# One layer of a recurrent and attention encoder in float32: all eight column tiles of the up projection's first half in Strassen quads

## The chip, the core and the metric

The kernel runs on one core of a Trainium2 chip. The metric is device time in microseconds of one execution, as the median of several runs. Five engines run side by side, each with its own queue of instructions in program order: TensorE (PE in the profile; its weight loads are PEld), VectorE (DVE), ScalarE (ACT), GpSimd (POOL) and SyncE (SP). An engine waits where it depends on another engine's result, on a transfer, or on a buffer that is still in use. SP issues the plain transfers of weights from device memory. POOL issues the accumulating ones, in which the DMA engines add the block that they read to what the destination holds.

## What is computed

The reference, cut to the part around the change (S = 512 tokens, D = 1024, D_FF = 4096, float32):

```python
x = x + concat(rms_norm(y_rnn), rms_norm(y_attn)) @ w_out     # w_out: 1024 x 1024
h = rms_norm(x, mlp_norm_g)
x = x + jnp.square(jax.nn.relu(h @ w_up)) @ w_down            # 1024 x 4096, 4096 x 1024
return rms_norm(x, final_norm_g)
```

Ahead of it stand the input projection, a gated linear recurrence in both directions, and a dilated attention of eight heads.

## The kernel before

**Split arithmetic.** Each float32 operand of a product is split in two fp32r numbers, `hi`, the rounded value, and `lo`, the remainder. `mm3` (lines 328 to 331) makes a product of three matmuls, hi*hi, hi*lo, lo*hi. For a weight chunk of 128x1024 the split is a cast `whi<-wraw` or `whi<-tw` on ACT (`conv_hi`, L274) and a subtraction `wlo<-...` on DVE (`conv_lo`, L282).

**The MLP.** It is computed in two halves of D_FF. Half 0's up projection (matmuls into `pu`) is followed by its down projection (into `pd`), then half 1's. An up half has 16 column tiles of 128, numbered f0. A plain column tile (`n0` to `n3`) takes eight contraction steps k of three matmuls of 128x512, all tokens, and one weight chunk. A quad f0 covers the four column tiles from f0 on by Strassen's scheme in Winograd's form: weights and activations are cut in blocks 11, 12, 21, 22 (two column groups by two halves of the contraction, two halves of the tokens), and seven products named `11`, `21`, `22`, `t1`, `t2`, `t3`, `t4` stand for eight. Each product is one weight chunk and 24 matmuls of 128x256. The operands t1 to t4 are sums of weight blocks: t1 = 12 + 11, t2 = t1 + 22, t3 = 12 + 22, t4 = t2 + 21 (signs are folded into the stored blocks). They are held in buffers `tw`. On the activation side the sums `hsum` stand against them, made from `hm`, the normed and transposed activations, and split to `hh` and `hl`; the activations themselves are split to `h2h` and `h2l`. Half 0 is four plain tiles and the quads 4, 8 and 12; half 1 is four quads (0, 8, 12, 4).

**What sets the order.** `STEPS` (L52) writes out the order of tiles and products in each half; chunks of weights follow it. During the step of chunk c, `feed` and `feed_q` cast and split chunk c+3, so ACT, DVE and TensorE run through the same list at a distance. In every quad but the first of half 0, `swap` converts t1 ahead of 11. A split frees the raw weights, and `conv_lo` then issues what may use that buffer next: `emit_dma` a plain load on SP into one of three `wraw` buffers, or, on POOL, the accumulation of 22 onto t1's buffer, which makes it t2 (L294). Where t3's or t4's sum needs the raw chunk 22 or 21, DVE adds it in place (L298, L303). `load_t` (L1196) takes one of four `tw` buffers, issues a plain load of block 12 on SP and the accumulations on POOL; its calls stand in `late`, a table of (f0, kind, n) that says beside which matmul group of which step something is done. `late` also places the activation sums, their splits (`split_h`), the squares of the residual stream for the final norms (`xt`, calling `x1_sq`), and `scale_neg`, which makes the negated norm factors `nr2`.

**Results of products.** `quad_evac` copies some products from PSUM to `v` on ACT (L1394) and adds later ones to them on DVE, `a<-v,pu` (L1404); relu and square follow on ACT or DVE. TensorE may start a product in a PSUM bank only when the one before it in that bank has been read. Products 11, t2, t3 and t4 of a quad share a bank.

**Start of half 0.** The output projection (into `pwo`) ends in `x1n<-pwo` on DVE (L1222). `h2_t` transposes `x1n` on TensorE into `pxt`, four 128x128 blocks for each k, ACT copies them to `h2h` and `hm`, DVE makes `h2l` (L1238). k = 0 to 3 stand before half 0's first product; k = 4 to 7 stand inside the first three plain tiles, which are interleaved.

Of the kernel before, what the change touches and what calls it, by code (L numbers as in the profile page):

```python
# [17 lines left out]
P = 128  # L18
# [23 lines left out]
for _n, _w in (("ag", 8), ("w0", 4), ("w1", 4), ("w2", 4), ("w3", 4), ("cb", 4),  # L42
# [13 lines left out]
ON_ACT = {(h, f, k) for h in range(2) for f in QUADS[h] if (h, f) != (0, 4) for k in ("21", "22", "t3", "t4")}  # L56

# [6 lines left out]
def up_steps(h):  # L64
    return [("n", int(s[1:])) if s[0] == "n" else (s.split(":")[1], int(s.split(":")[0])) for s in STEPS[h].split()]
# [44 lines left out]
def hybrid_kernel(ctx: ExitStack, tc, xw, xn, w_in, w_v, w_out, w_up, w_dn, gates, vecs, rel, onehot, fg, out):  # L110
# [165 lines left out]
    def conv_lo(i):  # L276
        if i < len(chunks):
# [13 lines left out]
            elif isinstance(c, tuple) and len(c) == 4:  # L291
# [4 lines left out]
                elif kind == "22":  # L296
                    t = raws[cq[h, f0, "t3"]]
                    nc.vector.tensor_tensor(t, t, r, op=OP.add)  # L298
                elif kind in ("t2", "21"):
# [896 lines left out]
    def load_t(half, n, f0):  # L1196
        t = work.tile([P, 1024], FT, name="tw", tag="tw", bufs=4)
        nc.sync.dma_start(t, ublock(half, "12", f0))
        for b in {"t1": ("11",), "t2": ("11", "22"), "t3": ()}[n]:
            nc.gpsimd.dma_start(t, ublock(half, b, f0), accum_op=OP.add)  # L1200
# [65 lines left out]
    BES["s1"].update({1: lambda: h2_t(0, "pj"), 2: lambda: h2_t(1, "pj"), 3: lambda: (conv_lo(C_WA + 8), h2_l(0))})  # L1266
    BES["22"].update({1: lambda: h2_t(2, "pj"), 2: lambda: (h2_t(3, "pj"), conv_lo(C_WA + 9)), 3: lambda: (h2_l(1), h2_l(2), h2_l(3))})
    for w in OSEQ:
# [7 lines left out]
        if w in ("s3", "s4", "s1"):  # L1276
            load_t(0, {"s3": "t1", "s4": "t2", "s1": "t3"}[w], 4)
# [4 lines left out]
    r2 = {}  # L1282

    def x1_sq(tt, n):
        s = small("ssn", 1)
        scr = g_("scr")
        act(scr, x1n[tt, n], AF.Square, accum_out=s)
        ssn[tt, n] = s
        if n == 1:
            r = consts.tile([P, 1], FT, name="r2_%d" % tt)  # L1290
            nc.vector.tensor_tensor(r, ssn[tt, 0], s, op=OP.add)
            nc.vector.tensor_scalar(r, r, 1.0 / D, EPS, op0=OP.mult, op1=OP.add)
            nc.vector.reciprocal(r, r)
            r2[tt] = r
# [35 lines left out]
    def up_evac(ff, p):  # L1330
        q, c = ff // 2, slice((ff % 2) * TH, (ff % 2 + 1) * TH)
        for t in range(2):
            if (q, t) not in rb:
                rb[q, t] = g_("a")
            act(rb[q, t][:, c], p[:, t * TH:(t + 1) * TH], AF.Relu)
        if ff % 2:
            for t in range(2):
                nc.vector.tensor_tensor(rb[q, t], rb[q, t], rb[q, t], op=OP.mult)
                rb_done.add((q, t))
            up_pair(q)  # L1340


# [5 lines left out]
    def h_sums(k):  # L1348
        m, c = k // 2, slice((k % 2) * TH, (k % 2 + 1) * TH)
        if k % 2 == 0:  # L1350
            for n in SUMS:
                hsum[n, m] = g_("hsum")
        a, b = hm.pop(k), hm.pop(k + 4)
        e, s2, s3, s4 = [hsum[n, m][:, c] for n in SUMS]
        nc.vector.tensor_tensor(e, b[:, right], a[:, right], op=OP.subtract)
        stt(s2, a[:, left], -1.0, e, op0=OP.mult, op1=OP.subtract)
        nc.vector.tensor_tensor(s3, a[:, left], a[:, right], op=OP.subtract)
        stt(s4, b[:, left], -1.0, s2, op0=OP.mult, op1=OP.subtract)
        if k % 2:
            for i, n in enumerate(SUMS):  # L1360
                nc.sync.dma_start(hsd[i][:, m * S:(m + 1) * S], hsum[n, m])
# [161 lines left out]
    nr2 = {}  # L1523
    for half in range(2):
        c0, cd = cu.get((half, 0)), cd_[half]
# [4 lines left out]
        start = 0  # L1530
        if half == 0:
            start = 3
            pu = [ps_("pu", "pj") for _ in range(start)]
            for k in range(KD):
                if k == 1:
                    for j in range(4, 8):
                        h2_t(j, "et" if j < 6 else "gs")
                        h2_l(j)
                for i in range(start):
                    mm3(pu[i], wk(c0 + i, k), h2k(k), k == 0, k == KD - 1)  # L1540
                    if i == 0:
# [12 lines left out]
            conv_hi(c0 + 5)
            conv_lo(c0 + 5)
            up_evac(2, pu[2])
        def scale_neg():
            nonlocal ts
            ts = big.tile([P, NQ, 1024], FT, name="ts", tag="bigA")
            for tt in range(4):  # L1560
                nr2[tt] = consts.tile([P, 1], FT, name="nr2_%d" % tt)
                nc.vector.tensor_scalar(nr2[tt], r2[tt], -1.0, None, op0=OP.mult)
# [5 lines left out]

        def up_tile(ff, late=()):
            p = ps_("pu", "pj")  # L1570
            c = cu[half, ff]
            for k in range(KD):
                mm3(p, wk(c, k), h2k(k), k == 0, k == KD - 1)
                feed(c, k)
                if (ff, k) in late:
                    late[ff, k]()
                if k in (1, 3, 5, 7):
                    op_next()
                if k in (5, 7):
                    next_a()  # L1580
            up_evac(ff, p)
# [3 lines left out]
        def up_step(kind, f0, late):  # L1585
            bank, keep = banks.setdefault(f0, {}), keeps.setdefault(f0, {})
            x = {"t1": "c", "22": "c", "21": "b"}.get(kind, "a")
            if x not in bank:
                bank[x] = ps_("pu", {"a": "pj" if (half, f0) == (1, 0) else "gs", "b": "pj", "c": "et"}[x])
            c = cq[half, f0, kind]  # L1590
            hi, lo = splits[c]
            for n in range(8):
# [9 lines left out]
                if n in (5, 7):  # L1602
                    op_next()
                if n == 6:
                    next_a()
            quad_evac(kind, f0, bank, keep, (half, f0, kind) in ON_ACT)

# [19 lines left out]
        for f0, f1 in zip(qs, qs[1:]):  # L1627
            late[f0, "t2", 0] = lambda f1=f1: load_t(half, "t1", f1)
            late[f0, "22", 0] = lambda f1=f1: load_t(half, "t3", f1)
        if half == 0:  # L1630
            late.update({(4, "11", 0): split_h("t2", 0), (4, "11", 5): split_h("t2", 1), (4, "t1", 1): split_h("22", 0), (4, "t1", 6): split_h("22", 1),
                         (3, 1): split_h("t3", 0), (3, 6): split_h("t3", 1),
# [183 lines left out]
```

## Time and profile before

| | |
|---|---|
| median of 3 runs | 531.61 us (530.47 to 531.9) |
| profiled execution | 532.29 us, span 530.5 us |
| busy, share of the span | TensorE 98%, DVE 81%, ACT 68%, POOL 13% |
| mean granted clock of TensorE | 0.997 of full speed |
| moved by DMA | 108.30 MB, mean 204 GB/s |
| accumulating transfers of w_up | 15 of 512 KB, median 8.3 us from issue to landing |

The span runs from the first to the last instruction; the 1.8 us beside it are start and end of the execution. A row of an engine's groups gives line, operation, output and inputs, shape and count, then busy time and mean duration of one in ns, then idle time ahead of it and what ended that. In rows of matmuls durations overlap, since they are pipelined. In a windows row stand, behind the stretch: its length and TensorE's busy time with count, then busy time and count of the weight loads, DVE, ACT and POOL, the granted clock, the DMA engines' busy share and GB/s. In timeline rows the first number is the start in us, the second the length; a number in brackets is a wait and what ended it.

### The profile page before, as it was taken

To read this page: it belongs to the slowest core of one execution; us is meant where nothing else is said; L and a number is where in the kernel's file an instruction comes from. 1 tells how busy PE (TensorE), PEld (TensorE's weight loads), DVE (VectorE), ACT (ScalarE), POOL (GpSimd) and SP (SyncE) were. 2 spreads that over 40 slices of the span, in tenths; PEclk is the share of its full clock that TensorE was granted. 3 is DMA by queue.
4 is the path that set the end of the run, shared out by engine and by line. 5 is a ranking of instruction groups with operands and counts; after the bars stand their busy time and mean duration, and the time that the engine had idled before them with its cause. 6 is when DMAs were issued, how large, how long until landed. Compare 5 with 4: busy or idle time off the path is not lost.

```text
span 530.5 us, 9181 instructions
## 1 busy us (share of the span) xinstructions
PE 521.1 (98%) x3495; PEld 446.4 (84%) x3495; DVE 431.0 (81%) x710; ACT 361.1 (68%) x569; POOL 66.8 (13%) x96
## 2 busy tenths in 40 slices
PE   8999999999999999999999999999999999999995
PEld 7855888877777878899999888888999999888884
DVE  5799589588779898898779986879756987987885
ACT  7566968578678867586477755575567677655654
POOL 3340000000202121001210222001101200131000
PEclk9999999999999999999999999999999999999998
DMA  8798165585567989948395999986968496799704
GB/s 309 256 236 217 41 152 159 164 150 179 105 220 153 331 196 256 371 146 229 100 214 144 228 272 274 311 289 140 291 209 228 107 223 207 163 299 263 174 1 159
DMA packets 35740, 108.30 MB, mean 204 GB/s; under 512 B 4109, under 2 KB 7082, under 8 KB 35696
## 3 DMA queue, kind: packets, MB, share of 16 engines
q1 hardware_dynamic: 26000, 74.66, 41.1%
q0 software_dynamic: 8784, 31.76, 32.1%
q10 hardware_dynamic: 912, 1.30, 1.3%
q8 instruction: 27, 0.44, 0.3%
q14 instruction: 17, 0.14, 0.1%
HBM read 98.24 MB, written 4.21 MB: 193 GB/s over the span
## 4 chain that ended last, share of the span: by engine, by line
PE 92%; ACT 2%; DMA 2%; DVE 2%; SPq 1%; issue 0%; DVEq 0%; ACTq 0%
PE pu L331 10%; PE pu L330 10%; PE pu L329 10%; PE pd L330 10%; PE pd L331 10%; PE pd L329 9%; PE pqk L329 3%; PE pqk L331 3%; PE pqk L330 3%; PE pt L841 2%; PE pav L928 2%; PE pv L329 1%; PE pn L787 1%; PE pp L331 1%; PE pp L329 1%; PE pp L330 1%
## 5 line engine op out<-in xcount | busy, mean ns | idle before, releaser
L282 DVE TENSOR_TENSOR wlo<-wraw,whi 128x1024 fp32r<-128x1024 f32 x72 | 87.8, 1221 | 26.4 <-ACT whi L274 26.2
L274 ACT ACTIVATE whi<-wraw 128x1024 fp32r<-128x1024 f32 x69 | 72.9, 1058 | 41.1 <-PE pd L331 20.5
L330 PE MATMUL pd<-wlo,ah 128*128 128x512 f32 (+1 forms) x195 | 75.4, 386 | 0.0
L329 PE MATMUL pd<-whi,ah 128*128 128x512 f32 (+1 forms) x195 | 75.3, 386 | 0.0
L331 PE MATMUL pd<-whi,al 128*128 128x512 f32 (+1 forms) x195 | 75.3, 386 | 0.0
L274 ACT ACTIVATE whi<-tw 128x1024 fp32r<-128x1024 f32 x40 | 42.3, 1059 | 38.0 <-DMA tw<-in_w_up_dram 11.1
L331 PE MATMUL pu<-hh,wlo 128*128 128x256 f32 x224 | 63.5, 284 | 0.0
L330 PE MATMUL pu<-hl,whi 128*128 128x256 f32 x224 | 63.5, 284 | 0.0
L329 PE MATMUL pu<-hh,whi 128*128 128x256 f32 x224 | 63.5, 283 | 0.0
L282 DVE TENSOR_TENSOR wlo<-tw,whi 128x1024 fp32r<-128x1024 f32 x40 | 48.9, 1223 | 17.9 <-ACT whi L274 17.9
L329 PE MATMUL pu<-h2h,whi 128*128 128x256 f32 (+1 forms) x200 | 60.2, 301 | 0.0
L331 PE MATMUL pu<-h2h,wlo 128*128 128x256 f32 (+1 forms) x200 | 60.1, 301 | 0.0
L330 PE MATMUL pu<-h2l,whi 128*128 128x256 f32 (+1 forms) x200 | 60.1, 301 | 0.0
L329 PEld LDWEIGHTS pu<-hh,whi 128*128 128x128 f32 x224 | 43.1, 192 | 0.0
L330 PEld LDWEIGHTS pu<-hl,whi 128*128 128x128 f32 x224 | 43.1, 192 | 0.0
L331 PEld LDWEIGHTS pu<-hh,wlo 128*128 128x128 f32 x224 | 43.1, 192 | 0.0
L329 PEld LDWEIGHTS pd<-whi,ah 128*128 128x128 f32 x195 | 36.7, 188 | 7.4
L330 PEld LDWEIGHTS pd<-wlo,ah 128*128 128x128 f32 x195 | 36.6, 188 | 7.3
L331 PEld LDWEIGHTS pd<-whi,al 128*128 128x128 f32 x195 | 36.7, 188 | 7.3
L274 ACT ACTIVATE whi<-ts 128x1024 fp32r<-128x1024 f32 x24 | 25.5, 1061 | 24.7 <-PE pd L331 18.5
L330 PEld LDWEIGHTS pu<-h2l,whi 128*128 128x128 f32 x200 | 38.3, 192 | 1.3
L331 PEld LDWEIGHTS pu<-h2h,wlo 128*128 128x128 f32 x200 | 38.3, 192 | 1.3
(286 smaller groups left out, 1232.8 us busy)
## 6 DMA issues: line engine op xcount, KB each, us to landing
wraw<-in_w_up_dram SPq DMA_DIRECT2D x25, 512.0 KB
ts<-in_w_dn_dram POOLq DMA_DIRECT2D x24, 512.0 KB, 13.5
wraw<-in_w_dn_dram SPq DMA_DIRECT2D x24, 512.0 KB
tw<-in_w_up_dram SPq DMA_DIRECT2D x15, 512.0 KB
tw<-in_w_up_dram POOLq DMA_DIRECT2D x15, 512.0 KB, 8.3
wraw<-in_w_in_dram SPq DMA_DIRECT2D x13, 512.0 KB
ts<-in_w_dn_dram SPq DMA_DIRECT2D x8, 512.0 KB
tw<-in_w_dn_dram SPq DMA_DIRECT2D x8, 512.0 KB
```

The lines of the kernel that those rows point to most:

```text
L274: act(hi, raws[i], AF.Copy)
L282: nc.vector.tensor_tensor(lo, r, f(splits[i][0]), op=OP.subtract)
L329: nc.tensor.matmul(o, lhsT=a[0], rhs=b[0], start=bool(first), stop=False, skip_group_check=on)
L330: nc.tensor.matmul(o, lhsT=a[0], rhs=b[1], start=False, stop=False, skip_group_check=on)
L331: nc.tensor.matmul(o, lhsT=a[1], rhs=b[0], start=False, stop=bool(last), skip_group_check=on)
L787: nc.tensor.matmul(pnear[p][e][r, o:o + k1 - k0], lhsT=q, rhs=raw[p, 1][halves[e], k0:k1], start=u == u0, stop=True, skip_group_check=True)
L841: nc.tensor.transpose(pt[:, i * P:(i + 1) * P], en[h][u][:, c * P:(c + 1) * P], ident)
L928: nc.tensor.matmul(o(half[e]), lhsT=v[:, h * DH:(h + 1) * DH], rhs=c(et[h, x]), start=first, stop=last, skip_group_check=True)
```

## The change

Half 0's plain column tiles go. In their place stands a quad 0, so that half 0 is four quads, 0, 4, 8 and 12:

```diff
 STEPS = (
-    "n0 n1 n2 4:11 4:t1 n3 4:t2 4:21 4:22 4:t3 8:11 8:t1 4:t4 8:t2 8:21 8:22 8:t3 12:11 12:t1 8:t4 12:t2 12:22 12:t3 12:21 12:t4",
+    "0:11 12:11 4:11 8:11 0:21 4:21 8:21 0:t1 4:t1 0:t2 0:22 0:t3 4:t2 0:t4 4:22 8:t1 4:t3 8:t2 4:t4 8:22 8:t3 12:t1 8:t4 12:t2 12:22 12:t3 12:21 12:t4",
...
-QUADS = ((4, 8, 12), (0, 8, 12, 4))
+QUADS = ((0, 4, 8, 12), (0, 8, 12, 4))
+EARLY = ((0, 0), (0, 4), (0, 8))
+ON_ACT = {(h, f, k) for h in range(2) for f in QUADS[h] if (h, f) != (0, 0) for k in ("21", "22", "t3", "t4")}
...
-        if kind == "11" and (h, f0) != (0, 4):
+        if kind == "11" and (h, f0) not in EARLY + ((0, 12),):
             swap[i], swap[i + 1] = i + 1, i
```

The products 11 and 21, which need no weight sums, come first for several quads, and `up_first` interleaves 0:11 and 12:11 at the start. Weight sums of half 0 that DVE made are made by accumulating transfers: t4 in the quads 0, 4 and 8 (21 onto t2's buffer) and t3 in the quads 0, 8 and 12 (22 onto 12). DVE keeps t3 of quad 4 and t4 of quad 12.

```diff
-                elif kind == "22":
+                elif kind == "22" and (h or f0 == 4):
                     t = raws[cq[h, f0, "t3"]]
                     nc.vector.tensor_tensor(t, t, r, op=OP.add)
+                elif (h, f0) in EARLY and kind == "t2":
+                    nc.gpsimd.dma_start(r, ublock(h, "21", f0), accum_op=OP.add)
+                    raws[cq[h, f0, "t4"]] = r
+                elif (h, f0) in EARLY and kind == "21":
+                    emit_dma()
...
     def load_t(half, n, f0):
         t = work.tile([P, 1024], FT, name="tw", tag="tw", bufs=4)
         nc.sync.dma_start(t, ublock(half, "12", f0))
-        for b in {"t1": ("11",), "t2": ("11", "22"), "t3": ()}[n]:
+        for b in {"t1": ("11",), "t2": ("11", "22"), "t3": () if half or f0 == 4 else ("22",)}[n]:
             nc.gpsimd.dma_start(t, ublock(half, b, f0), accum_op=OP.add)
...
-            load_t(0, {"s3": "t1", "s4": "t2", "s1": "t3"}[w], 4)
+            load_t(0, {"s3": "t1", "s4": "t2", "s1": "t3"}[w], 0)
...
+            late[0, "21", 0] = lambda: load_t(0, "t1", 4)
+            late[0, "21", 5] = lambda: load_t(0, "t1", 8)
+            late[0, "22", 5] = lambda: load_t(0, "t3", 4)
+            late[0, "t3", 0] = lambda: load_t(0, "t3", 8)
+            late[4, "t3", 0] = lambda: load_t(0, "t1", 12)
+            late[8, "t2", 5] = lambda: load_t(0, "t3", 12)
```

As built, the four `tw` buffers of half 0 are used in this order. One starts with an operand of the output projection, then holds 4:t1, 4:t2, 4:t4, then 12:t3. One holds 0:t1, then 8:t1, 8:t2, 8:t4. One holds 0:t2, 0:t4, then 8:t3. One holds 0:t3, then 4:t3, then 12:t1, 12:t2, 12:t4.

The accumulating transfers on POOL's queue, half 0's up projection, before (`tw` is a sum of blocks of w_up; the `ts` at the end belong to the down projection; L1200 is `load_t`, L294 makes t2):

```order
L1200 DMA tw<-in_w_up_dram 128x1024 x4
L294 DMA tw<-in_w_up_dram 128x1024
L1200 DMA tw<-in_w_up_dram 128x1024
L294 DMA tw<-in_w_up_dram 128x1024
L1513 DMA ts<-in_w_dn_dram 128x1024 x4
```

And after (L1202 is `load_t`, L291 makes t2, L297 makes t4, L1351 is `h_sum`):

```order
L1202 DMA tw<-in_w_up_dram 128x1024 x4
L1351 TENSOR_TENSOR hsum<-hm 128x256 x4
L1202 DMA tw<-in_w_up_dram 128x1024 x2
L291 DMA tw<-in_w_up_dram 128x1024
L297 DMA tw<-in_w_up_dram 128x1024 x2
L1202 DMA tw<-in_w_up_dram 128x1024
L291 DMA tw<-in_w_up_dram 128x1024
L297 DMA tw<-in_w_up_dram 128x1024
L1202 DMA tw<-in_w_up_dram 128x1024 x2
L291 DMA tw<-in_w_up_dram 128x1024
L1506 DMA ts<-in_w_dn_dram 128x1024 x4
```

In half 0 there were seven such transfers into `tw` and there are now fifteen. In the program's order the ones of after are 0:t1, two for 0:t2, 0:t3; then, behind four sums of activations, 4:t1 and 8:t1; 4:t2; 0:t4 and 4:t4; 8:t3; 8:t2; 8:t4; 12:t1 and 12:t3; 12:t2.

The activation sums of t3 move from DVE to POOL, and all sums are placed one by one in `late`:

```diff
-        nc.vector.tensor_tensor(s3, a[:, left], a[:, right], op=OP.subtract)
...
+            elif n == "t3":
+                nc.gpsimd.tensor_tensor(o, a[:, left], a[:, right], op=OP.subtract)
```

At the start of half 0 the order of transposes, `h2l` and weight splits changes. On TensorE the four groups of transposes k = 4 to 7 stood together after three products of k = 0 and now stand one by one in `up_first`.

```diff
-    BES["s1"].update({1: lambda: h2_t(0, "pj"), 2: lambda: h2_t(1, "pj"), 3: lambda: (conv_lo(C_WA + 8), h2_l(0))})
-    BES["22"].update({1: lambda: h2_t(2, "pj"), 2: lambda: (h2_t(3, "pj"), conv_lo(C_WA + 9)), 3: lambda: (h2_l(1), h2_l(2), h2_l(3))})
+    BES["s1"].update({1: lambda: h2_t(0, "pj"), 2: lambda: h2_t(1, "pj"), 3: lambda: (h2_t(2, "pj"), h2_l(0))})
+    BES["22"].update({0: lambda: (h2_t(3, "pj"), conv_lo(C_WA + 8)), 1: lambda: conv_hi(C_WA + 9), 3: lambda: h2_l(1)})
```

DVE at the end of the output projection and the start of half 0, before (the two `wlo` are splits of the first chunks of w_up; `hm_2400`, `hm_2411`, `hm_2441` are k = 0, 1, 2):

```order
L1222 SCALAR_TENSOR_TENSOR x1n_2416<-pwo_2381,nrc_2257,x1_1764 128x512
L282 TENSOR_TENSOR wlo_2418<-wraw_2231,whi_2385 128x1024
L1238 TENSOR_TENSOR h2l_2393<-hm_2400,h2h_2392 128x512
L1222 SCALAR_TENSOR_TENSOR x1n_2433<-pwo_2380,nrc_2257,x1_1465 128x512
L282 TENSOR_TENSOR wlo_2454<-wraw_2349,whi_2428 128x1024
L1222 SCALAR_TENSOR_TENSOR x1n_2461<-pwo_2381,nrc_2257,x1_1467 128x512
L1238 TENSOR_TENSOR h2l_2393<-hm_2411,h2h_2392 128x512
L1238 TENSOR_TENSOR h2l_2393<-hm_2441,h2h_2392 128x512
```

And after (`hm_2400`, `hm_2411`, `hm_2424`, `hm_2439` are k = 0 to 3):

```order
L1224 SCALAR_TENSOR_TENSOR x1n_2416<-pwo_2381,nrc_2257,x1_1764 128x512
L1240 TENSOR_TENSOR h2l_2393<-hm_2400,h2h_2392 128x512
L279 TENSOR_TENSOR wlo_2441<-wraw_2231,whi_2385 128x1024
L1224 SCALAR_TENSOR_TENSOR x1n_2448<-pwo_2380,nrc_2257,x1_1465 128x512
L1224 SCALAR_TENSOR_TENSOR x1n_2458<-pwo_2381,nrc_2257,x1_1467 128x512
L1240 TENSOR_TENSOR h2l_2393<-hm_2411,h2h_2392 128x512
L1240 TENSOR_TENSOR h2l_2393<-hm_2424,h2h_2392 128x512
L1240 TENSOR_TENSOR h2l_2393<-hm_2439,h2h_2392 128x512
L279 TENSOR_TENSOR wlo_2489<-wraw_2349,whi_2450 128x1024
```

The split of `wraw_2349` stood ahead of the last `x1n` and of the `h2l` of k = 1, and stands behind four `h2l` now.

DVE in the last third of half 0's up projection, before (`tw_3048` is 12:t1 in the first row and 12:t2 in the last, `tw_2790` is 8:t4, `a_3185<-v_3009,pu_2939` the sum of product 8:t3, `pu_2939` the bank that 8:t4 writes next; the four `nr2` are the negated norm factors):

```order
L282 TENSOR_TENSOR wlo_3096<-tw_3048,whi_3088 128x1024
L1562 TENSOR_SCALAR nr2_0_3103<-r2_0_2721 128x1
L1562 TENSOR_SCALAR nr2_1_3105<-r2_1_2847 128x1
L1562 TENSOR_SCALAR nr2_2_3107<-r2_2_2889 128x1
L1562 TENSOR_SCALAR nr2_3_3109<-r2_3_2965 128x1
L1404 TENSOR_TENSOR a_3117<-v_2975,pu_3078 128x512
L282 TENSOR_TENSOR wlo_3138<-wraw_2884,whi_3130 128x1024
L1404 TENSOR_TENSOR a_3151<-v_3076,pu_2977 128x512
L282 TENSOR_TENSOR wlo_3172<-tw_2790,whi_3162 128x1024
L1404 TENSOR_TENSOR a_3185<-v_3009,pu_2939 128x512
L282 TENSOR_TENSOR wlo_3207<-tw_3048,whi_3197 128x1024
```

And after (`tw_3113` is 12:t1, then 12:t2; `tw_2689` is 8:t4; `a_3287<-v_3108,pu_2618` is the sum of 8:t3, and `pu_2618` the bank that 8:t4 writes next; `r2_3243` and `nr2_3244` are the norm factors):

```order
L279 TENSOR_TENSOR wlo_3203<-tw_3113,whi_3193 128x1024
L279 TENSOR_TENSOR wlo_3237<-tw_2689,whi_3228 128x1024
L1293 TENSOR_TENSOR r2_3243<-ssn_2962,ssn_2997 128x4
L1294 TENSOR_SCALAR r2_3243<-r2_3243 128x4
L1295 RECIPROCAL r2_3243<-r2_3243 128x4
L1296 TENSOR_SCALAR nr2_3244<-r2_3243 128x4
L1397 TENSOR_TENSOR a_3255<-v_3182,pu_3077 128x512
L279 TENSOR_TENSOR wlo_3274<-tw_3113,whi_3266 128x1024
L1397 TENSOR_TENSOR a_3287<-v_3108,pu_2618 128x512
```

The sum of 8:t3 stood ahead of the split of 12:t2, and stands behind it now.

The squares' sums of the residual stream are kept in two tiles of four columns, and the norm factors are made for all four token tiles together:

```diff
+    def x1_r():
+        r, m = [consts.tile([P, 4], FT, name=n) for n in ("r2", "nr2")]
+        nc.vector.tensor_tensor(r, ssn[0], ssn[1], op=OP.add)
+        nc.vector.tensor_scalar(r, r, 1.0 / D, EPS, op0=OP.mult, op1=OP.add)
+        nc.vector.reciprocal(r, r)
+        nc.vector.tensor_scalar(m, r, -1.0, None, op0=OP.mult)
```

They stood in two places, as single columns, `r2` with the squares and `nr2` in `scale_neg`, and all stand in `scale_neg` now, beside 8:22. Half 1 and both down projections are not edited.

More of the change, by code (lines that the diff above doesn't have):

```diff
@@ L64, in up_steps @@
 def up_steps(h):
-    return [("n", int(s[1:])) if s[0] == "n" else (s.split(":")[1], int(s.split(":")[0])) for s in STEPS[h].split()]
+    return [(s.split(":")[1], int(s.split(":")[0])) for s in STEPS[h].split()]
 def up_quadrants(w, f):
@@ L1559, in scale_neg @@
             ts = big.tile([P, NQ, 1024], FT, name="ts", tag="bigA")
-            for tt in range(4):
-                nr2[tt] = consts.tile([P, 1], FT, name="nr2_%d" % tt)
-                nc.vector.tensor_scalar(nr2[tt], r2[tt], -1.0, None, op0=OP.mult)
+            x1_r()
         def next_a():
@@ L1626, in hybrid_kernel @@
         qs = QUADS[half]
-        for f0, f1 in zip(qs, qs[1:]):
+        for f0, f1 in zip(qs, qs[1:]) if half else ():
             late[f0, "t2", 0] = lambda f1=f1: load_t(half, "t1", f1)
```

157 lines of the change are left out of this document (60 added, 97 removed).

## The prediction

> **What bounds the kernel now.** I read the page's busy times and chain first, then the stretch of the edit by windows, then TensorE's timeline at its ends.
>
> ```profile
> PE 521.1 (98%) x3495; PEld 446.4 (84%) x3495; DVE 431.0 (81%) x710; ACT 361.1 (68%) x569; POOL 66.8 (13%) x96
> PE 92%; ACT 2%; DMA 2%; DVE 2%; SPq 1%; issue 0%; DVEq 0%; ACTq 0%
> 206.70:290.70 84.00, 84.00 (x617) 80.15 (x616) 71.44 (x108) 57.07 (x93) 7.02 (x8) 1.00 0.73 205
> 291.00:348.00 57.00, 57.00 (x253) 47.22 (x252) 47.78 (x59) 35.20 (x46) 10.50 (x12) 1.00 1.01 269
> ```
>
> TensorE carries the chain and is busy for all of the half-0 up stage (206.70 to 290.70), at full clock. Every microsecond of matmuls removed there is a microsecond won, and every wait put there one lost. DVE, the next engine, has 71.44 of 84 us. DMA engines are 0.73 busy there, and 1.01 in the down stage behind it.
>
> ```profile
> 204.44 0.60 PE L1232 MATMUL pxt<-ident,x1n 128*128 128x128 f32 x4
> 204.80 0.48 PE L329 MATMUL pwo<-whi,oh 128*128 128x512 f32 x1
> 206.47 0.40 PE L331 MATMUL pwo<-whi,ol 128*128 128x512 f32 x1
> 206.71 0.39 PE L329 MATMUL pu<-h2h,whi 128*128 128x512 f32 x1
> 208.77 1.91 PE L1232 MATMUL pxt<-ident,x1n 128*128 128x128 f32 x16
> 210.43 0.47 PE L329 MATMUL pu<-h2h,whi 128*128 128x512 f32 x1
> 224.82 0.28 PE L329 MATMUL pu<-h2h,whi 128*128 128x256 f32 x1
> 290.75 0.40 PE L329 MATMUL pd<-whi,ah 128*128 128x512 f32 x1
> ```
>
> Durations overlap, so the price is the distance between starts. From 206.71 to 224.82 stand 72 wide matmuls (three plain tiles) and 16 transposes of 1.66 us (208.77 to 210.43): (18.11 - 1.66) / 72 = 0.2285 us. From 224.82 to 290.75 stand the fourth plain tile (24 x 0.2285 = 5.48) and three quads of 7 x 24 narrow matmuls: (65.93 - 5.48) / 504 = 0.120 us.
>
> **What is removed on the path.** Four plain tiles, 96 x 0.2285 = 21.9 us, become a quad, 168 x 0.120 = 20.2 us. The transposes in four groups of four cost 0.36 us (204.44 to 204.80) and some 0.08 in the next matmul, 1.8 for 1.66. Gain: 1.7 us, and no more. The Trainium skill, TensorE: Matmul & The Clock Gate, Back-to-back issue gap, gives N/2.4 + 2.5 ns, 216 and 109 ns here; by that estimate the gain would be 20.7 - 18.3 = 2.4 us. The trace's distances are longer and decide.
>
> **DVE and ACT.** Prices by form:
>
> ```profile
> L282 DVE TENSOR_TENSOR wlo<-tw,whi 128x1024 fp32r<-128x1024 f32 x12 | 14.7, 1222 | 4.1 <-ACT whi L274 4.1
> L1404 DVE TENSOR_TENSOR a<-v,pu 128x512 f32<-128x512 f32 x9 | 6.1, 679 | 1.3 <-PE pu L331 1.2
> L303 DVE TENSOR_TENSOR tw<-tw,wraw 128x1024 f32<-128x1024 f32 x3 | 3.7, 1218 | 0.0
> L1338 DVE TENSOR_TENSOR a<-a 128x512 f32<-128x512 f32 x4 | 2.6, 685 | 0.0
> L1357 DVE TENSOR_TENSOR hsum<-hm 128x256 f32<-128x256 f32 x4 | 1.7, 418 | 0.0
> L1292 DVE TENSOR_SCALAR r<-r 128x1 f32<-128x1 f32 x4 | 0.6, 155 | 0.1
> L274 ACT ACTIVATE whi<-tw 128x1024 fp32r<-128x1024 f32 x12 | 12.7, 1062 | 9.1 <-PE pu L330 6.9 <-DVE tw L298 1.6 <-DVE tw L303 0.7
> L1394 ACT ACTIVATE v<-pu 128x512 f32<-128x512 f32 x9 | 5.4, 605 | 5.1 <-PE pu L331 5.1
> L1375 ACT ACTIVATE hh<-hsum 128x512 fp32r<-128x512 f32 x8 | 5.3, 660 | 4.4 <-DVE hsum L1355 4.4
> L1412 ACT ACTIVATE a<-a 128x512 f32<-128x512 f32 x5 | 3.1, 616 | 0.0
> L1335 ACT ACTIVATE a<-pu 128x256 f32<-128x256 f32 x8 | 2.5, 388 | 1.0 <-PE pu L331 1.0
> ```
>
> DVE: 28 weight splits for 25, +3.7; two weight sums for six, -4.9; four t3 sums to POOL, -1.7; four plain squares gone, -2.7; three quad sums, +2.0; norm factors four tiny operations for sixteen, -12 x 0.155 = -1.9. Together -5.5 us. ACT: +3 casts 3.2, +3 copies 1.8, +8 relus and squares 4.9, -8 half relus 3.1: +6.8 us, to 64 of 82. Both stay under TensorE, so all of this is worth nothing on average; the norm factors lie under matmuls and are used only in the down stage. If DVE's cover went, its 66 of 82 us would still leave 16 us.
>
> **The start.** TensorE needs h2l of k = 1 at its 14th matmul: 206.71 + 13 x 0.12 = 208.3.
>
> ```profile
> 206.31 1.22 DVE L282 TENSOR_TENSOR wlo<-wraw,whi 128x1024 fp32r<-128x1024 f32 x1
> 207.44 0.75 DVE L1222 SCALAR_TENSOR_TENSOR x1n<-pwo,nrc,x 128x512 f32<-128x512 f32 x1
> 208.10 1.89 DVE L1238 TENSOR_TENSOR h2l<-hm,h2h 128x512 fp32r<-128x512 f32 x3
> ```
>
> That weight split is moved behind them (the first DVE excerpt), so the last x1n can start when the last pwo matmul ends (206.87), and h2l is there 0.66 + 0.69 later, at 208.2. I take 0; at before's times (208.10 + 0.69 = 208.8) it would be 0.5.
>
> **DMA, the term that decides.** Half 0 goes from 20 plain and 7 accumulating 512 KB transfers to 21 and 15.
>
> ```profile
> 240.35 0.33 SPq L1198 DMA_DIRECT2D tw<-in_w_up_dram  x1
> 242.21 0.86 POOL L294 DMA_DIRECT2D tw<-in_w_up_dram  x1 [36.83 <-DVE r L1292]
> 244.19 0.86 POOL L1200 DMA_DIRECT2D tw<-in_w_up_dram  x1 [1.11 <-DMA tw<-in_w_up_dram]
> DMA to landing us min/median/max: 5.2/5.3/7.4
> 262.37 0.86 POOL L294 DMA_DIRECT2D tw<-in_w_up_dram  x1 [17.32 <-DVE nr L1562]
> 262.91 3.90 POOL L1513 DMA_DIRECT2D ts<-in_w_dn_dram  x4
> DMA to landing us min/median/max: 9.3/12.8/17.2
> L1513 POOL DMA_DIRECT2D ts<-in_w_dn_dram x4: 1221/1752/2286, 262.9 to 264.5; - x4
> ```
>
> A plain transfer issued at 240.35 released POOL at 244.19: 3.8 us. An accumulating one alone lands in 5.3. Several queue: the one of 262.37 landed at 267.6, and the four behind it between 262.91 + 9.3 = 272.2 and 264.5 + 17.2 = 281.7, so each takes 14.1 / 4 = 3.5 us more (3.2 to 4.6). A split is 1.06 on ACT and 1.22 on DVE, 2.3.
>
> The changed kernel strings these on one chain, since POOL issues in order and an operand's buffer is another's before it. Without stalls, 4:11 starts at 206.71 + 48 x 0.12 + 1.7 = 214.2, and each later step 24 x 0.12 = 2.88 on:
> - 8:11 ends at 220.0; ACT copies it (0.6), splits t1 (0.66) and casts 0:t1 (1.06), since that cast's buffer waits for 8:11; DVE, one hl behind, has split it at 223.9. It frees the buffer of 8:t1.
> - 8:t1: plain load 3.8, then POOL issues its addition at 227.7, and behind it those of 4:t2 and 0:t4, which could have gone earlier. Landings: 233.0, 236.5, 240.0.
> - 0:t4 split: 242.3. It frees the buffer of 8:t3. Plain load to 246.1; its addition lands at 251.4, 8:t2's behind it at 254.9.
> - 8:t2 split: 257.2. Then additions of 8:t4 (262.5) and 12:t1 (266.0) in POOL's order.
> - 12:t1 split: 268.3. Only then 12:t2's addition, landed 273.6; split 275.9.
> - DVE's sum of 8:t3 stands behind that split (second DVE excerpt): 276.6. 8:t4 writes the same bank, and TensorE reaches it at 214.2 + 20 x 2.88 = 271.8.
>
> In before the sum of 8:t3 stood ahead of the split of 12:t2. So TensorE waits 4.8 us in all (0.7 of it already at 0:t4, whose bank waits for a sum behind the split of 0:t4). Bounds: at 3.2 for each of the four queued transfers 1.2 less, at 4.6 4.4 more; nothing below full cover, 0. I take 3.5, measured in an up stage like this one. SP loads wait for the same splits and raw weights behind them, but those come up to three steps ahead.
>
> Sum: -1.7 + 4.8 = +3.1 us. The profiled execution took 532.29 us (span 530.5), 0.7 above the median of 531.61; against it 535.4, against the median 534.7.
>
> **Rivals.**
> - Faster or the same: the chain is covered. The additions are 0.5 us apart in issue; did they land so, four gaps of 3.5 would shrink and 8:t4 would not wait. Then 531.6 - 1.7 = 529.9. It decides at 3.1 us of chain saved, gaps of some 2.7 us, to be no slower, and at 2.3 to be clean. For it: half 1 has landings late enough that ACT waits for them, and TensorE is still full. Against: no gap of the burst is under 3.2 on average, and half 1 has two additions a quad, not four.
>
> ```profile
> ACT whi L274 <- DMA tw<-in_w_up_dram: 9.2, 3, 5.1
> ```
>
> - DMA throughput. The queues' shares price a transfer of 0.524 MB:
>
> ```profile
> q1 hardware_dynamic: 26000, 74.66, 41.1%
> q0 software_dynamic: 8784, 31.76, 32.1%
> ```
>
> 0.411 x 530.5 / 74.66 = 2.92 us a MB plain, 5.36 accumulating. Eight additions and one load more are 8 x 2.81 + 1.53 = 24 us on the 61 of this stage (0.73 x 84), 85 in 82. The 3 us over would go into the down stage, which is full at 1.01: -1.7 + 3 = +1.3, 532.9, if none is absorbed. Against: the 1.01 there went with no stall.
> - POOL against DVE. The four t3 sums run on POOL at 205.4 and later, beside h2l. If a DVE operation had to wait for one, h2l of k = 1 is late by it. Nearest rows:
>
> ```profile
> L176 POOL TENSOR_TENSOR pl<-pl,z 128x8 f32<-128x8 f32 x8 | 2.6, 328 | 0.6
> L416 POOL TENSOR_TENSOR rcol<-rv,mhalf 128x4 f32<-128x4 f32 x2 | 3.0, 1506 | 14.6 <-DVE rv L413 14.6
> ```
>
> One such sum costs 0.3 to 1.5: alone it leaves 530.2 to 531.4, no measurable change. The Trainium skill, SBUF — State Buffer, SBUF: two separate sides, says that DVE and GpSimd share a port pair under an exclusive lock, held for a whole instruction; no row of before has the two side by side on large tiles.
>
> **The numbers.** A measurement of this kernel tells a change from none at about 0.3%, 1.6 us. Chances: the late chain 0.48 (534.7; its own range 533.5 to 539.1); throughput 0.12 (532.9); POOL against DVE alone 0.10 (530.8); covered 0.30 (529.9, of which 0.19 beyond 0.3%). The throughput case falls within 0.3% for the most part. That makes faster 0.20, same 0.29, slower 0.51. The range reaches from the covered case less half the spread of the three runs, 529.9 - 0.7, to the chain with gaps of 4.3, 534.7 + 4 x 0.8: 529.2 to 537.9.
>
> **What would show it.** Step by step: narrow matmuls at 0.120 and no 128x512 form left of pu; the first pd matmul at 293.9 (289.1 if covered); TensorE's wait of some 4 us ahead of pu<-h2h at 8:t4, released by DVE's sum of 8:t3; ACT's cast of 12:t2 released by a DMA; accumulating transfers of tw at a median near 8 us to landing. DVE near 66 us in the stage. Wrong if additions queue at under 2.7 us, if the cast of 0:t1 is done much before 222, or if waits at the start exceed 1 us.

## The result: 19 us slower, and the profile after

The changed kernel takes 550.63 us (548.95 to 552.64, 4 runs) against 531.5: a ratio of 1.0362, 95% interval 1.0342 to 1.0382. The sign was forecast, the size (534.7, at most 537.9) was not. The profiled execution is the fastest of the four, 548.95 us with a span of 547.1, so the trace holds 16.6 of the 19 us (530.5 before). Of the experiments below, `t3_on_dve_tw6` and `t1_12_first` had one execution of over 1000 us each (1327.82 and 1043.34), and the figures given for them are of the other three.

The page of the changed kernel, busy times, the queue of accumulating transfers, and the chain that ended last by engine:

```profile
PE 525.1 (96%) x3567; PEld 452.2 (83%) x3567; DVE 429.4 (78%) x692; ACT 366.8 (67%) x575; POOL 78.6 (14%) x108
q0 software_dynamic: 9936, 35.95, 35.0%
PE 46%; DMA 5%; DVE 1%; ACT 1%; issue 0%; POOL 0%; DVEq 0%; ACTq 0%
```

TensorE lost two points, and DVE has no more to do than before. The chain is followed back to 254.86 us only (its shares add up to some 53%), so they can't be set beside those of before. By windows, the changed half-0 up stage, then three stretches of it:

```profile
206.10:308.00 101.90, 87.55 (x690) 86.04 (x689) 69.65 (x91) 62.22 (x97) 16.49 (x19) 0.95 0.82 214
206.70:220.00 13.30, 11.37 (x81) 11.02 (x80) 9.49 (x12) 7.31 (x12) 2.73 (x3) 0.87 1.04 289
250.00:265.00 15.00, 12.33 (x101) 11.95 (x100) 6.35 (x7) 4.05 (x8) 1.73 (x2) 1.00 0.75 185
280.00:295.00 15.00, 8.61 (x59) 8.43 (x58) 8.57 (x13) 8.92 (x13) 4.08 (x5) 0.77 1.05 208
```

The second stretch in the kernel before:

```profile
206.70:220.00 13.30, 13.30 (x68) 11.26 (x67) 11.09 (x22) 8.30 (x15) 0.00 (x0) 1.00 1.02 322
```

What TensorE waited for from 200 to 310 us (total, times, longest), DVE's sums first of all:

```profile
PE pu L331 <- DVE a L1397: 11.0, 4, 6.4
PE pu L333 <- DVE wlo L279: 2.0, 2, 1.2
PE pu L332 <- DVE h2l L1240: 0.7, 1, 0.7
PE pu L331 <- ACT whi L271: 0.7, 1, 0.7
```

The stage, first `pu` to first `pd` matmul, went from 84.0 to 101.8 us. What follows it, up to the end of the last operation of an engine that computes, is 235.6 us long in both kernels: the whole loss is here. I add up the distances between starts of matmuls: those above 0.5 us are waits, 15.6 us over the 0.12 of a matmul; those between 0.16 and 0.25 are matmuls at a lower granted clock (0.87 and 0.77 above), 3.3 us over. Without both, 101.8 - 15.6 - 3.3 = 82.9 us, 1.2 less than before: the gain in matmuls is there. Of the 15.6 us, 2.25 stand at the start, 1.07 ahead of 8:21, and 12.3 at four products: 0:t4 (2.4), 8:t2 (1.8, in two waits), 4:t4 (1.6) and 8:t4 (6.6). The first matmuls behind them, but for the longest wait, which follows below:

```profile
230.20 0.36 PE L331 MATMUL pu<-h2h,whi 128*128 128x256 f32 x1 [0.91 <-DVE a L1397]
252.84 0.36 PE L331 MATMUL pu<-h2h,whi 128*128 128x256 f32 x1 [2.27 <-DVE a L1397]
265.29 0.39 PE L331 MATMUL pu<-hh,whi 128*128 128x256 f32 x1 [0.70 <-ACT whi L271]
270.84 0.36 PE L331 MATMUL pu<-h2h,whi 128*128 128x256 f32 x1 [1.39 <-DVE a L1397]
```

The chain of waits ahead of the longest wait, and the matmuls behind it:

```profile
254.86 9.24 DMA tw<-in_w_up_dram
264.18 1.07 ACT whi L271
265.27 1.24 DVE wlo L279
266.79 0.54 POOL tw L297
267.33 9.68 DMA tw<-in_w_up_dram
277.04 1.07 ACT whi L271
278.13 1.24 DVE wlo L279
279.65 6.20 DMA tw<-in_w_up_dram
285.93 1.06 ACT whi L271
288.16 0.69 DVE a L1397
288.99 0.55 PE pu L331
289.54 0.21 PE pu L332
...
293.02 0.12 PE pu L332
```

These are 8:t2's addition and split, 12:t1's behind 8:t4's on POOL, 12:t2's, and then the sum of 8:t3 that 8:t4 waits for: the end of the chain of the prediction, in its order and at its place. Its transfers take 9.2, 9.7 and 6.2 us from issue to landing; the first two queue behind 8:t3's and 8:t4's additions and land 4.6 and 4.8 us after them. For 3.4 us behind the wait, matmuls follow each other at 0.21 us. All additions into `tw` from 206 to 295 us (minimum, median, maximum from issue to landing; 5.2, 5.3 and 7.4 before):

```profile
DMA to landing us min/median/max: 5.3/6.4/12.0
```

The whole chain, as the prediction worked it out and as the trace has it:

| | worked out | trace | later by |
|---|---|---|---|
| 8:11 ends on TensorE | 220.0 | 223.4 | 3.4 |
| 0:t1 is split | 223.9 | 229.5 | 5.6 |
| 8:t1's addition is issued | 227.7 | 234.4 | 6.7 |
| 0:t4's addition lands | 240.0 | 246.2 | 6.2 |
| 8:t3's addition is issued | 246.1 | 253.1 | 7.0 |
| 8:t2's addition lands | 254.9 | 264.1 | 9.2 |
| 12:t1's addition lands | 266.0 | 277.0 | 11.0 |
| 12:t2's addition lands | 273.6 | 285.9 | 12.3 |
| the sum of 8:t3 is made | 276.6 | 288.9 | 12.3 |
| TensorE comes to 8:t4 | 271.8 | 282.4 | 10.6 |

Ahead of the split of 0:t1, ACT waited for a plain load of weights, the chunk of 4:21:

```profile
222.32 1.06 ACT L271 ACTIVATE whi<-wraw 128x1024 fp32r<-128x1024 f32 x1 [2.04 <-DMA wraw<-in_w_up_dram]
228.24 1.22 DVE L279 TENSOR_TENSOR wlo<-tw,whi 128x1024 fp32r<-128x1024 f32 x1
```

### The profile page after: what moved, and what is told of

Its sections match the earlier page's. It is cut to its first block, busy times and chain, and to the rows that moved or that the text cites. A ratio compares the mean times of both kernels' runs of the same rounds, so it can differ in the third digit from the quotient of the medians.

```text
span 547.1 us, 9345 instructions
## 1 busy us (share of the span) xinstructions
PE 525.1 (96%) x3567; PEld 452.2 (83%) x3567; DVE 429.4 (78%) x692; ACT 366.8 (67%) x575; POOL 78.6 (14%) x108
## 4 chain that ended last, share of the span: by engine, by line
PE 46%; DMA 5%; DVE 1%; ACT 1%; issue 0%; POOL 0%; DVEq 0%; ACTq 0%
PE pd L333 9%; PE pd L331 9%; PE pd L332 9%; PE pu L331 6%; PE pu L333 6%; PE pu L332 6%; DMA tw<-in_w_up_dram 5%; ACT whi L271 1%; DVE wlo L279 0%; DVE a L1397 0%; POOL tw L297 0%; DVE x1n L1481 0%; DVE ot L1490 0%; DVE x1n L1472 0%; DVE scr L1482 0%
## 5 line engine op out<-in xcount | busy, mean ns | idle before, releaser
L333 PE MATMUL pu<-hh,wlo 128*128 128x256 f32 x256 | 72.6, 283 | 0.8 <-DVE wlo L279 0.8
L331 PE MATMUL pu<-hh,whi 128*128 128x256 f32 x256 | 72.6, 284 | 0.7 <-ACT whi L271 0.7
L332 PE MATMUL pu<-hl,whi 128*128 128x256 f32 x256 | 72.5, 283 | 0.0
L331 PE MATMUL pu<-h2h,whi 128*128 128x256 f32 x192 | 56.2, 293 | 11.0 <-DVE a L1397 11.0
L333 PE MATMUL pu<-h2h,wlo 128*128 128x256 f32 x192 | 55.5, 289 | 1.2 <-DVE wlo L279 1.2
L332 PE MATMUL pu<-h2l,whi 128*128 128x256 f32 x192 | 55.4, 289 | 0.7 <-DVE h2l L1240 0.7
L333 PEld LDWEIGHTS pu<-hh,wlo 128*128 128x128 f32 x256 | 49.2, 192 | 1.0 <-DVE wlo L279 1.0
L331 PEld LDWEIGHTS pu<-hh,whi 128*128 128x128 f32 x256 | 49.2, 192 | 0.9 <-ACT whi L271 0.9
L332 PEld LDWEIGHTS pu<-hl,whi 128*128 128x128 f32 x256 | 49.2, 192 | 0.0
L331 PEld LDWEIGHTS pu<-h2h,whi 128*128 128x128 f32 x192 | 38.0, 198 | 11.7 <-ACT a L1405 6.6
```

The source lines that it names most:

```text
L331: nc.tensor.matmul(o, lhsT=a[0], rhs=b[0], start=bool(first), stop=False, skip_group_check=on)
L332: nc.tensor.matmul(o, lhsT=a[0], rhs=b[1], start=False, stop=False, skip_group_check=on)
L333: nc.tensor.matmul(o, lhsT=a[1], rhs=b[0], start=False, stop=bool(last), skip_group_check=on)
```

## Experiments

"Stage" is first `pu` to first `pd` matmul of the profiled run, "rest" what follows, measured as above (235.6 to 236.1 us unless said). Ratios are to runs of the kernel before on the same chip.

**First set: the start, the buffers, the order.** In the changed kernel the start shows this on DVE, POOL and TensorE (timeline):

```profile
203.89 4.13 DVE L279 TENSOR_TENSOR wlo<-wraw,whi 128x1024 fp32r<-128x1024 f32 x1
204.12 4.47 POOL L1351 TENSOR_TENSOR hsum<-hm 128x256 f32<-128x256 f32 x4
208.08 0.39 PE L333 MATMUL pu<-h2h,wlo 128*128 128x256 f32 x1 [1.23 <-DVE wlo L279]
210.00 0.39 PE L332 MATMUL pu<-h2l,whi 128*128 128x256 f32 x1 [0.70 <-DVE h2l L1240]
```

```diff
-                nc.gpsimd.tensor_tensor(o, a[:, left], a[:, right], op=OP.subtract)
+                nc.vector.tensor_tensor(o, a[:, left], a[:, right], op=OP.subtract)
```

> The four activation sums of t3 go back from POOL to DVE, nothing else. Theory (POOL's sums block DVE at the start): in the changed kernel a weight split on DVE took 4.13 us instead of 1.22 beside the four POOL sums, TensorE then waited 1.43 for it and 0.91 for h2l and ran some 30 matmuls at 0.21 apart instead of 0.12. Without that the half-0 up products start some 4 to 5 us earlier against the old end, and the chain of transfers with them: 550.6 - 4.5 = 546. Rival (the start is late because of the new order of splits, x1n and h2l on DVE, not because of POOL): DVE gets 1.7 us more of sums there, so 550 to 552.

Measured: 552.61, ratio 1.0404 (1.0388 to 1.0419), stage 105.9. The split is back at 1.22 us and the first waits are gone, but TensorE meets others 13 us later:

```profile
202.79 1.22 DVE L279 TENSOR_TENSOR wlo<-wraw,whi 128x1024 fp32r<-128x1024 f32 x1
221.99 1.06 ACT L271 ACTIVATE whi<-wraw 128x1024 fp32r<-128x1024 f32 x1 [5.07 <-DMA wraw<-in_w_up_dram]
231.21 0.55 PE L331 MATMUL pu<-h2h,whi 128*128 128x256 f32 x1 [3.95 <-DVE a L1397]
```

POOL did hold DVE, as the theory said; the gain went into a wait for a plain load of weights, which neither theory had.

```diff
-    NG = 48
+    NG = 44
...
-        t = work.tile([P, 1024], FT, name="tw", tag="tw", bufs=4)
+        t = work.tile([P, 1024], FT, name="tw", tag="tw", bufs=6)
```

> Six tw buffers in place of four, taken from four of the 48 512-column buffers; the order on TensorE, DVE, ACT and POOL is the same. Theory (a chain of buffer reuse, each link a load, an addition and a split): 8:t1, 8:t3 and 12:t1 are loaded early and additions no longer stand behind late ones, so TensorE's waits from 228 us on, 14 us with the slow matmuls behind the longest, go almost wholly: 550.6 - 13 = 537.5. Rival (the DMA engines cannot move fifteen additions in this stage, whatever the buffers): at most 4 us are won, 547 or more.

> Both edits. Theory (two independent causes, the POOL sums and the chain of buffers): the two gains add, 550.6 - 4.5 - 13 = 533, within 2 us. If the late chain is started by the late start, they overlap and the sum is nearer 537. If throughput is what limits, 543 or more.

Measured: 554.39 (1.039 to 1.0451) and 555.18 (1.0418 to 1.051). Here the rest is 243.1 and 242.4 us, 7 longer, presumably for the four buffers taken away, which was not tried alone; so these two are read by their stages, 100.9 and 99.4. In `tw6` the waits from 250 us on fell from 12.9 to 8.2 between starts, those at 224 to 233 rose from 1.2 to 4.4. Buffer reuse is not what the 19 us are.

```diff
-                feed(c, n)
+                sum_first = (half, kind, f0, n) == (0, "t3", 8, 4)
+                if not sum_first:
+                    feed(c, n)
...
             quad_evac(kind, f0, bank, keep, (half, f0, kind) in ON_ACT)
+            if (half, kind, f0) == (0, "t3", 8):
+                conv_lo(c + 3)
```

> DVE makes the sum of 8:t3 before it splits 12:t2, as in the kernel before; nothing else. Theory: the wait of 6.4 us ahead of 8:t4 is only this order, since the sum's inputs are ready at 282.4. TensorE starts 8:t4 at about 282.9 and then waits at 12:t2 for its split (288.2 us): 285.8 to 288.2, so 3.5 to 4 us are won, 1 to 2 more if the matmuls behind a shorter wait are not slow: 545 to 547. Rival (8:t4 was itself late, or the split of 12:t2 moves later by as much): 550.

Measured: 549.73 (1.0327 to 1.0364), stage 100.7. The longest wait went from 6.7 to 2.5 us between starts, and one of 2.6 appeared that ends at 304: the order alone is not it.

**Second set: the additions and the loads beside them.**

```diff
-                elif kind == "22" and (h or f0 == 4):
+                elif kind == "22":
...
-"t3": () if half or f0 == 4 else ("22",)
+"t3": ()
```

> The weight sums of t3 of quads 0, 8 and 12 are made by DVE again (1.22 us each) and not by accumulating transfers; twelve additions in half 0 and not fifteen. Theory A (a late addition holds up ACT's casts, DVE's splits behind them and the additions queued on POOL): 8:t3's addition, 6.4 us from issue to landing, leaves the chain ahead of 8:t2, so the wait ahead of 8:t4 shrinks by about that: 550.6 - 5 = 545.5. Theory B (what counts is the stretch from 203 to 225 us, in which the DMA engines are full and plain loads come late): only 0:t3's addition leaves that stretch, and TensorE waited for DVE there anyhow: 549 to 551.

Measured: 542.75 (1.0176 to 1.0272), stage 94.6: 7.9 us for three additions.

```diff
+        def new_ts():
+            nonlocal ts
+            ts = big.tile([P, NQ, 1024], FT, name="ts", tag="bigA")
+            nc.vector.memset(ts[:, :, 0:1], 0.0)
```

`new_ts` is called beside 4:22, `scale_neg` no longer makes `ts`, and the activation sums of t3 are on DVE as in `t3_on_dve`.

> As the run with the activation sums of t3 on DVE (552.6), and the four plain loads of ts for the down stage, issued from 202 to 206 there, may be issued only after the step 4:22, at about 250 us. Theory B (DMA engines full at the start; the cast of a plain w_up chunk waited 5.1 us for its load and TensorE 7.2 us in all between 220 and 231): 2.1 MB at 2.92 us a MB, 6.1 us of DMA time, leave that stretch, the casts come up to 6 us earlier and the waits there go: 552.6 - 7 = 545.5, and the gain of the sums on DVE becomes visible. Theory A (the chain of additions sets the end): the late waits take up what the early ones give back, 550 to 553.

Measured: 547.39 (1.0277 to 1.0318), 5.2 less than its partner, stage 100.8. Theory B holds at the start: with 2.1 MB out of the way, the waits from 220 to 232 fell from 7.2 to 1.6. The four loads then stood at 262 to 267 beside 8:t4's addition, which took 9.8 us.

```diff
-                    nc.gpsimd.dma_start(r, ublock(h, "21", f0), accum_op=OP.add)
...
-"t3": () if half or f0 == 4 else ("22",)
+"t3": ()
```

> The six accumulating transfers that took the place of DVE's sums (t4 of quads 0, 4, 8, t3 of quads 0, 8, 12) are left out, and so are their sums, so those products are of other operands. Order, buffers and all else stay. This prices these transfers together. Theory A: TensorE's waits from 250 us on, 12.5 us and the slow matmuls behind the longest, mostly go, the additions of t1 and t2 remain: 550.6 - 10 = 540.5. Theory B: the early stretch is as it was, so 546 or more.

Measured: 535.76 (1.007 to 1.0104), stage 88.6, 0.76 DMA share. Six additions are worth 14.9 of the 19 us.

> Four edits together: activation sums of t3 on DVE, weight sums of t3 on DVE, ts loaded late, six tw buffers. If A and B both hold, each for its part, the early waits (7 us and more in the run with sums on DVE) and most of the late ones go: 535 to 539. If only one holds, 543 to 547.

Measured: 551.03 (1.0349 to 1.0383): stage 95.9, but 242.8 us of rest, as with six buffers above.

**Third set: with four buffers.** One call moved:

```diff
-            late[4, "t3", 0] = lambda: load_t(0, "t1", 12)
+            late[4, "22", 0] = lambda: load_t(0, "t1", 12)
```

> From the changed kernel, one call is moved: 12:t1's load stands two steps earlier in the program, so on POOL its addition stands ahead of 8:t4's and not behind it. Theory A (POOL's order is a link of the chain): the load of 12:t1 was issued at 255.5 and its addition at 267.3, behind 8:t4's, which waited for the split of 8:t2; issued some 5 us after the load, it lands about 10 us earlier, 12:t2's addition some 5 earlier, and the wait of 6.4 us ahead of 8:t4 shrinks to 1 to 2: 550.6 - 5 = 545.5. Rival (ACT's casts, in order behind the late 8:t2, 8:t3 and 12:t1, set it, not POOL): 549 or more.

Measured: 546.25 (1.0231 to 1.0329; 543.13 to 548.42), stage 99.7. POOL's order is a link, worth 4.4 us by the medians; with this spread the expected 5 is not excluded. In the profiled run the wait ahead of 8:t4 went from 6.7 to 3.6 between starts, and those at 225 to 232 rose from 1.2 to 3.9.

> The kernel without six additions (535.8; the sums of these operands are left out), and the start mended as well: activation sums of t3 on DVE, the four loads of ts some 30 us later. Theory: it had 2.7 us of waits left at 206 to 209 and 3.3 later. Without the first, 535.8 - 3.5 = 532.3, about the kernel before. Rival (the start's waits turn into waits for loads a few us later): 535 or more.

Measured: 535.38 (1.0047 to 1.0102), 0.4 less than without the mended start: the rival. 8:t2's addition, 5.8 us there, now had the `ts` loads beside it and took 8.8.

> Four tw buffers as in the changed kernel, and four edits: both kinds of t3 sums on DVE, ts loaded later (from step 0:t3 on), 12:t1's addition ahead of 8:t4's. From the run with weight sums of t3 on DVE (542.8): 4 us of start and 3 to 4 of the wait ahead of 8:t4: 535 to 536. If the pieces give back to each other, 539 to 541.

Measured: 539.4 (1.0141 to 1.0188), stage 93.7: the pieces give back to each other.

> As the run before in this set, and 8:21 stands behind 8:t2, so DVE makes t4 of quad 8 from raw blocks as it does in quad 12; ten additions. Theory A (each late addition costs): 2 to 3 us less than that run, 533. Rival (activation sums needed one step earlier now make waits at 0:t1): 1 to 3 us more.

Measured: 539.96 (1.0144 to 1.0187), stage 93.3: eleven additions, one less than the run before and not ten as written, and nothing won; a wait of 3.1 us between starts for activation sums came, up to 234.7.

**Fourth set: what makes an addition dear.** `free_add4` issues four of the additions into a spare buffer, `no_add4` leaves them out; four operands lack a sum in both:

```diff
-                    pass
+                    nc.gpsimd.dma_start(spare[:, f0 // 4, :], ublock(h, "21", f0), accum_op=OP.add)
...
-                pass
+                nc.gpsimd.dma_start(spare[:, 3, :], ublock(half, b, f0), accum_op=OP.add)
```

> From the changed kernel: the four additions that lie in the chain (t4 of quads 0, 4, 8; t3 of quad 8) are left out, with their sums; four ACT copies of 1.06 us into a spare buffer and ts loaded after 8:t2 are added as in its partner. Chain theory and throughput theory both give a stage of 89 to 92 us against 101.8 (no six additions: 88.6).

> The same kernel, and the same four additions are issued from the same places, 512 KB each, but into a spare buffer that nobody reads. Chain theory (each addition costs because a cast waits for it and all casts, splits and sums behind it stand in order): close to its partner without them, at most 2 us more. Throughput theory (the engines' and the queue's time that they take): 8 to 12 us more than the partner, near the changed kernel. If queueing of the remaining additions behind them is half of it: 4 to 6.

Measured: 541.53 (1.0174 to 1.0212), stage 95.6, and 549.19 (1.0311 to 1.0353), stage 102.0. Four transfers that nobody waits for cost 7.7 us. What the chain costs, neither says. The whole stage by windows, without the four and with them:

```profile
206.00:301.50 95.50, 85.55 (x689) 84.62 (x688) 69.34 (x92) 65.22 (x101) 12.74 (x14) 0.96 0.77 207
```

```profile
206.10:308.00 101.90, 88.34 (x689) 87.61 (x688) 68.04 (x92) 65.89 (x101) 15.52 (x18) 0.92 0.83 214
```

The timelines where they part, SP's plain loads of 4:t3 and 8:t3 and DVE's sum onto the first, without and with:

```profile
240.55 5.15 SPq L1201 DMA_DIRECT2D tw<-in_w_up_dram  x2
247.72 1.22 DVE L296 TENSOR_TENSOR tw<-tw,wraw 128x1024 f32<-128x1024 f32 x1
```

```profile
239.63 5.98 SPq L1201 DMA_DIRECT2D tw<-in_w_up_dram  x2
252.91 1.23 DVE L296 TENSOR_TENSOR tw<-tw,wraw 128x1024 f32<-128x1024 f32 x1 [5.19 <-DMA tw<-in_w_up_dram]
```

A plain load of 512 KB, which in the kernel before released POOL after 3.8 us, took some 13 (239.63 to just ahead of 252.91) beside three additions, DVE waited 5.19 for it, and TensorE stood 5.1 us at 249.8. That one wait and the slow matmuls behind it are the difference: TensorE is 5.2 us behind the run without the four when it starts 0:t4 (254.88 for 249.68), and 6.5 at the end of the stage. In the changed kernel this load cost no wait: 4:t4's and 8:t3's additions, issued at 232.9 and 233.4 here, are issued at 245.6 and 253.1 there, and DVE makes the sum at 250.89 without waiting. So the pair shows that additions which nobody waits for can cost as much, through a load beside them, and not that this is where the changed kernel lost its time. The Trainium skill, DMA: Bandwidth & Descriptors, Issuing engines are not separate DMA queues, says that transfers run on the same 16 engines and interleave whichever engine issued them; the trace agrees.

> As combo4 (539.4), but the four loads of ts may go from about 212 us on and not from 244, where they stood beside 8:t2's addition, which then took 9.3 us. The DMA engines were 0.70 busy from 206.7 to 220 there. If the late collision is what is left: 536 to 537. If the early plain loads come late again: 540 or more.

Measured: 537.8 (1.0095 to 1.0137), stage 90.3: the best of the kernels with all four quads, 6.5 us behind the kernel before.

> The kernel before with one part of the change alone: the norm factors of the four token tiles made together, four small operations in place of sixteen. All theories: 1.9 us of DVE time under matmuls, no change within 0.3%: 531.4, 530.5 to 532.

Measured: 531.18 against 531.26, ratio 0.9998 (0.9989 to 1.0008), 10 runs. No change, as expected.

**Last: as few additions as can be.** Half 0's order is rewritten so that each 21 stands beside its t2 (ahead of it but for 12:21), and DVE makes all t3 and t4:

```diff
+    "0:11 12:11 4:11 8:11 0:21 0:t1 4:t1 0:t2 0:22 0:t3 4:21 4:t2 0:t4 4:22 8:t1 4:t3 4:t4 8:21 8:t2 8:22 8:t3 12:t1 8:t4 12:t2 12:21 12:22 12:t3 12:t4",
```

> All t3 and t4 sums of half 0 on DVE (each 21 beside its t2 in the order of steps), activation sums of t3 on DVE, ts from about 212 us on: nine additions in half 0 where the kernel before had seven and the changed one fifteen. Throughput theory: from combo5 (stage 90.3 us, 12 additions, waits 5.9) three additions less and 21s at their t2: stage 84 to 86, 531 to 534. If DVE's 75 us of work in 82 or activation sums needed two steps earlier now bind, 90 or more, 537 and up.

Measured: 540.03 (1.0134 to 1.0185), stage 94.3. Windows of the stage's second stretch, of `combo5` first and then of this run:

```profile
220.00:235.00 15.00, 14.71 (x123) 14.53 (x122) 14.96 (x24) 9.38 (x15) 2.65 (x3) 1.00 0.99 295
```

```profile
220.00:235.00 15.00, 12.43 (x90) 12.22 (x90) 14.93 (x26) 8.45 (x13) 1.73 (x2) 0.85 1.03 310
```

DVE is full in both rows, 14.96 and 14.93 of 15 us, and so, or nearly, are the DMA engines. What differs is TensorE, which waited in this run for DVE's split of an activation sum:

```profile
PE pu L332 <- DVE hl L1371: 2.6, 1, 2.6
```

That is the second case of the expectation, for this stretch; what its other two waits (2.1 us up to 261.3 and 2.5 up to 297.1, both released by a sum on DVE) come from was not followed up. None of these kernels beats the one before.

## Why the prediction was right or wrong

- **Gain of 1.7 us in matmuls: right.** 1.2 in the changed kernel (82.9 for 84.0), 1.9 in `combo5` (90.3 less 5.9 of waits and 2.2 of slow matmuls: 82.1).
- **DVE and ACT under cover on average, norm factors worth nothing: right** (`before_x1r`, and DVE at 69.7 of 101.9 us).
- **The start, taken at 0 and at most 0.5: wrong.** 2.25 us of waits between starts and some ten matmuls at 0.21. The rival named the cause, POOL against DVE, and priced it at 0.3 to 1.5; the split took 2.9 longer. It is also not worth its own size: without it the loads bind (`t3_on_dve`).
- **The late chain, +4.8: the mechanism, the order and the two places named were right, its size was not.** This is the step that failed. The waits on the chain are 12.3 us, above the 9.2 that its own widest bound allowed: 2.4 at 0:t4 and 6.6 at 8:t4, which it named (0.7 and 4.1), and 3.3 at 8:t2 and 4:t4, which it did not. The chain begins 5.6 us later than worked out: 3.4 because 8:11 ends late, and the rest goes with ACT's wait of 2.0 for a plain load, for which the working had no term. Its links then take 6.7 us more. The plain loads ahead of 8:t1's and 8:t3's additions take 4.9 and 4.6 for 3.8; the additions of 8:t3 and 12:t2, which queue behind no other, 6.4 and 6.2 for 5.3; those of 8:t2 and 12:t1 land 4.6 and 4.8 after the one ahead, for 3.5. The first burst, of 8:t1, 4:t2 and 0:t4, landed 3.2 and 3.3 apart, as worked out. That the additions bring most of the loss is shown: with three of them made on DVE instead the kernel is 7.9 us faster, with six left out 14.9.
- **The rival "DMA throughput", at a chance of 0.12 and a price of 1.3 us, holds at the start of the stage.** Its work was nearly right, 85 us; the trace has 0.82 x 101.9 = 83.6. What failed is that it was set against the whole stage, 85 in 82. The work isn't spread evenly. From 206 to 220 the engines are full (1.04), the `ts` loads among the work; full they were before too (1.02), but plain tiles wanted a chunk in 5.48 us and quad steps want one every 2.88, so now loads come late, and the waits for them all but go when the `ts` loads go (`ts_late`). That the later links take longer for the same reason is likely but not shown: the engines are 0.75 busy from 250 to 265 and 0.63 from 265 to 280.
- **Not in the sum at all: the lower granted clock**, 3.3 us, and the wait ahead of 8:21, 1.07. With them the stage adds up: -1.2 + 2.25 + 1.07 + 12.3 + 3.3 = 17.7, measured 101.8 - 84.0 = 17.8.
- **Of the signs named**, narrow matmuls at 0.120, the wait at 8:t4 released by DVE's sum, the cast of 12:t2 released by a DMA and DVE near 66 us came true or nearly (69.7). The median landing of 8 us depends on where one counts: 6.4 in this stage, and 8.0 over the whole program, where it was 8.3 before. The first pd matmul stood at 307.9 and not at 293.9. "Waits at the start exceed 1 us" was named as what would make it wrong, and did.

Open: how the 15 us of the six additions divide between the chain's waiting and the time that they take from other transfers, and so why the later links run longer. The four of `free_add4` bunch together since they wait for nothing, so their 7.7 us is not the same four transfers' share in the changed kernel.

## What to carry to other kernels

An accumulating transfer that takes a sum from a vector engine is not free because that engine was busy: price it in DMA engine time (2.8 us for 512 KB by the queue's share in the kernel before) in the very stretch where it stands, together with each plain load that has a date there, and not over the stage. On a chain of buffers, each link that is late makes the next one late: ask of every duration what else was in flight where it was read, and work out the chain's start, with its loads, as carefully as its links. When the one waiting engine is relieved, ask which load its delay had been hiding.

## What the hardware showed that I had not expected

- Four 128x256 operations on POOL held one DVE operation for 2.9 us (4.13 for 1.22). The Trainium skill, SBUF — State Buffer, SBUF: two separate sides, says so of DVE with two inputs in SBUF against a POOL operation that reads it; the trace agrees, and the hold was more than one POOL operation long (4.47 / 4 = 1.12 us).
- The granted clock was lower around some waits: 0.77 over 280 to 295 us, with matmuls 0.21 apart for 3.4 us behind a wait of 6.4. It was 0.85 and 0.93 in stretches whose longest gaps were 2.9 and 2.3 us (`dve_sums`, `combo5`), and 1.00 over 250 to 265 us in the changed kernel with a gap of 2.5 at 252.8, so the length of a gap alone does not tell.
- A plain 512 KB load took some 13 us beside three accumulating ones, 3.8 in the kernel before.
